# A batched matmul on one core: all loads first, all stores after, with every output kept on chip

## The chip, the cores and the metric

The kernel runs on one core of a Trainium2 chip. The metric is the device time of one execution in microseconds (us).

## The reference

```python
def setup_inputs():
    batch, m, k, n = 16, 512, 512, 512
    return {
        "a": np.random.randn(batch, k, m).astype(np.float32),
        "b": np.random.randn(batch, k, n).astype(np.float32),
    }

def reference(a, b):
    return np.matmul(a.transpose(0, 2, 1), b).astype(np.float32)
```

Per batch, 1 MiB of `a` and 1 MiB of `b` come in and 1 MiB goes out: 48 transfers of 1 MiB, 50.33 MB (33.55 in, 16.78 out).

## The kernel before

One queue (the sync engine, SP) issues every load and every store but one small first write. Loads run six batches ahead of stores (`LAG`). VectorE (DVE) casts each input to bfloat16, TensorE (PE) multiplies into the result memory PSUM, and ScalarE (ACT) evacuates that, which means that it copies the result into an output tile in the on-chip memory SBUF. HBM is the memory outside, where the inputs and the output are.

```python
    LAG = 6
    NL = 5            # float32 input slots
    NB = 2            # bfloat16 slots
    NO = LAG + 2      # output slots
    H = MO // 2
    ...
        def load(i):
            j = i % NL
            if i >= NL:
                nc.sync.wait_ge(s_acast, i - NL + 2)
            nc.sync.dma_start(a_ts[j][:], a_v[i]).then_inc(s_a[j], 16)
            nc.sync.dma_start(b_ts[j][:], b_v[i]).then_inc(s_b[j], 16)

        def store(i):
            if i == 0:
                nc.sync.wait_ge(s_w, 16)
            nc.sync.wait_ge(s_ev1, i + 1)
            nc.sync.dma_start(out_v[i], o_ts[i % NO][:]).then_inc(s_o[i % NO], 16)

        for i in range(LAG):
            load(i)
        for i in range(batch):
            if i + LAG < batch:
                load(i + LAG)
            store(i)
    ...   # DVE: cast a, cast b; PE: 16 matmuls a batch
        for i in range(batch):          # ACT
            if i >= NO:
                nc.scalar.wait_ge(s_o[i % NO], 16 * (i // NO))
            for h in range(H):
                nc.scalar.wait_ge(s_mm, H * i + h + 1)
                nc.scalar.copy(out=o_ts[i % NO][:, 2 * h:2 * h + 2, :],
                               in_=ps_ts[(i % NB) * H + h][:]
                ).then_inc(s_ev1 if h else s_ev0, 1)
```

So from the seventh batch of loads on the queue holds: load `a`, load `b`, store, load `a`, load `b`, store, and so on. The kernel in full:

## Time and profile before

| before | |
|---|---|
| time, median of the first 3 executions | 126.58 us (126.41 to 127.03) |
| span of the profiled execution | 124.4 us |
| bytes moved | 50.33 MB by the main queue |
| busy share of the span | PE 55%, DVE 32%, ACT 27%, DMA engines 97.1% |

These lines are from the page of the kernel before. The first is the busy time of PE, with its share of the span. The next three show the span in 40 slices: the granted PE clock in tenths, the busy share of the DMA engines in tenths, and what these moved. Then come the main DMA queue (packets, MB, share of 16 engines) and the three costliest kinds of work (busy us, mean ns of one, idle time before them and what ended it).

```profile
PE 68.8 (55%) x256; PEld 29.5 (24%) x256; DVE 39.3 (32%) x32; ACT 33.6 (27%) x33; POOL 0.4 (0%) x5
...
PEclk9999999999999996799855999586799859999655
DMA  3999999999999999999999999999999999999991
GB/s 47 424 429 424 424 424 421 424 421 424 424 414 424 432 421 432 419 424 419 429 408 427 432 419 429 427 427 424 421 432 427 421 419 421 421 421 427 437 419 42
...
q1 hardware_dynamic: 6912, 50.33, 97.1%
...
L100 PE MATMUL ps<-bbf,abf 128*128 128x512 bf16 x256 | 68.8, 430 | 42.1 <-PEq L97 42.1
L120 ACT COPY o<-ps 128x1024 f32<-128x1024 f32 x32 | 32.3, 1013 | 64.6 <-PE ps L100 64.6
...
L86 DVE CAST abf<-a 128x2048 bf16<-128x2048 f32 x16 | 19.6, 1227 | 48.6 <-DMA a<-in_a_dram 48.6
```

The DMA row is what to look at: 9 in every slice but the first and the last, at some 424 GB/s. The compute engines spend most of their time waiting, and the casts wait for DMA. This kernel is bound by its transfers. The Trainium skill, "HBM Reference", section "Specifications (TRN2)", gives about 358 GB/s as the per-core share and says that a core streaming alone reaches about 425; the 424 here agree with the latter.

The next lines are from the timeline of DVE: start, duration, engine, line, operation, and in brackets how long the engine was idle and what ended that. They are the `a` casts of batches 8 to 11, and those of batches 14 and 15.

```profile
50.76 1.23 DVE L86 CAST abf<-a 128x2048 bf16<-128x2048 f32 x1 [3.76 <-DMA a<-in_a_dram]
...
58.16 1.23 DVE L86 CAST abf<-a 128x2048 bf16<-128x2048 f32 x1 [3.76 <-DMA a<-in_a_dram]
...
66.03 1.23 DVE L86 CAST abf<-a 128x2048 bf16<-128x2048 f32 x1 [4.23 <-DMA a<-in_a_dram]
...
73.41 1.23 DVE L86 CAST abf<-a 128x2048 bf16<-128x2048 f32 x1 [3.74 <-DMA a<-in_a_dram]
...
95.60 1.23 DVE L86 CAST abf<-a 128x2048 bf16<-128x2048 f32 x1 [3.78 <-DMA a<-in_a_dram]
...
103.37 1.23 DVE L86 CAST abf<-a 128x2048 bf16<-128x2048 f32 x1 [4.13 <-DMA a<-in_a_dram]
```

The casts follow the transfers, so their starts are a clock for the stream. Most batches take 7.40 us (3.146 MB, 425 GB/s). Two take longer: 58.16 to 66.03 is 7.87 us, and 95.60 to 103.37 is 7.77 us. Together they are some 0.84 us over.

### The profile page before, as it was taken

The page shows a single profiled execution, that of the slowest core. Times are in us where ns is not written, and L with a number is a line of the kernel's source. Part 1 is how long each engine was busy: PE and PEld are TensorE (multiplying, and loading weights), DVE is VectorE, ACT ScalarE, POOL GpSimd, SP SyncE. Part 2 cuts the span into 40 slices and gives each one's busy share as a digit, 9 for nine tenths or more (in the row PEclk, how much of TensorE's full clock was granted, in tenths as well). Part 3 has the DMA queues.
Part 4 walks back from the last instruction along what each step waited for, and adds up shares of the span by engine and source line. Part 5 has one row for each costly group of instructions (what it writes and reads, how often), then busy time and mean ns, then how long its engine had stood idle before and what let it go on. Part 6 is the DMA issues. An engine that isn't in the chain of part 4 may idle for free. (4 is left out here: it accounts for less than half of the span.)

```text
span 124.4 us, 762 instructions
## 1 busy us (share of the span) xinstructions
PE 68.8 (55%) x256; PEld 29.5 (24%) x256; DVE 39.3 (32%) x32; ACT 33.6 (27%) x33; POOL 0.4 (0%) x5
## 2 busy tenths in 40 slices
PE   0007989595775907947099561957937095560000
PEld 0002344252342403323033220313323032220000
DVE  0055345534653061333403333061332503300000
ACT  0000564633524330425003360240325106060000
POOL 1000000000000000000000000000000000000000
PEclk9999999999999996799855999586799859999655
DMA  3999999999999999999999999999999999999991
GB/s 47 424 429 424 424 424 421 424 421 424 424 414 424 432 421 432 419 424 419 429 408 427 432 419 429 427 427 424 421 432 427 421 419 421 421 421 427 437 419 42
DMA packets 7056, 50.40 MB, mean 405 GB/s; under 512 B 784, under 2 KB 912, under 8 KB 912
## 3 DMA queue, kind: packets, MB, share of 16 engines
q1 hardware_dynamic: 6912, 50.33, 97.1%
q10 hardware_dynamic: 144, 0.07, 0.2%
HBM read 33.55 MB, written 16.84 MB: 405 GB/s over the span
## 5 line engine op out<-in xcount | busy, mean ns | idle before, releaser
L100 PE MATMUL ps<-bbf,abf 128*128 128x512 bf16 x256 | 68.8, 430 | 42.1 <-PEq L97 42.1
L120 ACT COPY o<-ps 128x1024 f32<-128x1024 f32 x32 | 32.3, 1013 | 64.6 <-PE ps L100 64.6
L100 PEld LDWEIGHTS ps<-bbf,abf 128*128 128x128 bf16 x256 | 29.5, 120 | 80.9 <-issue 63.3
L86 DVE CAST abf<-a 128x2048 bf16<-128x2048 f32 x16 | 19.6, 1227 | 48.6 <-DMA a<-in_a_dram 48.6
L88 DVE CAST bbf<-b 128x2048 bf16<-128x2048 f32 x16 | 19.6, 1227 | 19.1 <-DMA b<-in_b_dram 19.1
L120 ACT ACT_TABLE_LOAD x1 | 1.3, 1283 | 13.7 <-PE ps L100 13.7
L111 POOL MEMSET o<- 128x128 f32 x1 | 0.2, 204 | 0.5 <-SPq L57 0.5
L137 POOL MEMSET const-bfloat16-1.0<- 128x1 bf16 x1 | 0.1, 101 | 0.0
L137 POOL MEMSET const-uint8-127<- 128x1 uint8 x1 | 0.1, 101 | 0.0
L137 POOL MEMSET const-float32-0.0<- 128x1 f32 x1 | 0.1, 98 | 0.2 <-issue 0.2
L137 POOL MEMSET const-float32-1.0<- 128x1 f32 x1 | 0.1, 98 | 0.0
## 6 DMA issues: line engine op xcount, KB each, us to landing
a<-in_a_dram SPq DMA_DIRECT2D x16, 1024.0 KB, 22.2
b<-in_b_dram SPq DMA_DIRECT2D x16, 1024.0 KB, 24.3
out_dram<-o SPq DMA_DIRECT2D x16, 1024.0 KB, 26.1
out_dram<-o ACTq DMA_DIRECT2D x1, 64.0 KB, 5.0
```

The source lines that it names most:

```text
L86: nc.vector.tensor_copy(out=abf_ts[i % NB][:], in_=a_ts[i % NL][:]).then_inc(s_acast, 1)
L88: nc.vector.tensor_copy(out=bbf_ts[i % NB][:], in_=b_ts[i % NL][:]).then_inc(s_bcast, 1)
L100: mm = nc.tensor.matmul(ps_ts[u * H + mo // 2][:, mo % 2, :], a_m[:, ko, mo, :], bbf_ts[u][:, ko, :], start=(ko == 0), stop=(ko == KO - 1),)
L111: nc.gpsimd.memset(o_ts[0][:, 0, 0:P], 0.0).then_inc(s_z, 1)
L120: nc.scalar.copy(out=o_ts[i % NO][:, 2 * h:2 * h + 2, :], in_=ps_ts[(i % NB) * H + h][:]).then_inc(s_ev1 if h else s_ev0, 1)
L137: nc = _bacc.Bacc("TRN2", target_bir_lowering=False, num_devices=1)
```

## The change

The intent is to stop mixing loads and stores. All 16 outputs (16 tiles of 8 KB per partition) stay in SBUF, so stores can wait; to make room, the float32 input slots go from five to three. The queue issues all 32 loads and then all 16 stores. ACT never waits for an output slot. The diff, without its changes of blank lines:

```diff
-    LAG = 6
-    NL = 5
+    NL = 3
     NB = 2
-    NO = LAG + 2
     H = MO // 2
...
-    o_ts = [pool.tile([P, MO, N], f32, name=f"o{j}") for j in range(NO)]
+    o_ts = [pool.tile([P, MO, N], f32, name=f"o{j}") for j in range(batch)]
...
-    s_o = [tc.alloc_semaphore(f"s_o{j}") for j in range(NO)]
+    s_o = tc.alloc_semaphore("s_o")
...
-            nc.sync.dma_start(out_v[i], o_ts[i % NO][:]).then_inc(s_o[i % NO], 16)
+            nc.sync.dma_start(out_v[i], o_ts[i][:]).then_inc(s_o, 16)
 
-        for i in range(LAG):
+        for i in range(batch):
             load(i)
         for i in range(batch):
-            if i + LAG < batch:
-                load(i + LAG)
             store(i)
-        for j in range(NO):
-            nc.sync.wait_ge(s_o[j], 16 * len(range(j, batch, NO)))
+        nc.sync.wait_ge(s_o, 16 * batch)
...
         for i in range(batch):
-            if i >= NO:
-                nc.scalar.wait_ge(s_o[i % NO], 16 * (i // NO))
             for h in range(H):
                 nc.scalar.wait_ge(s_mm, H * i + h + 1)
                 nc.scalar.copy(
-                    out=o_ts[i % NO][:, 2 * h:2 * h + 2, :], in_=ps_ts[(i % NB) * H + h][:]
+                    out=o_ts[i][:, 2 * h:2 * h + 2, :], in_=ps_ts[(i % NB) * H + h][:]
                 ).then_inc(s_ev1 if h else s_ev0, 1)
```

## The prediction

> **What bounds the kernel now.** The DMA engines. In the page's slices the DMA row is at 9 from the second to the second-last slice, at 408 to 437 GB/s; queue q1 carries 50.33 MB in 97.1% of the 16 engines' span. 50.33 MB at 424 GB/s are 118.7 us of a 124.4 us span; the rest is latency at both ends. The Trainium skill, "DMA: Bandwidth & Descriptors", section "Bandwidth", gives 425 GB/s as measured for a large load; this trace agrees. No compute engine is near: PE 55%, DVE 32%, ACT 27%.
>
> **What the change does.** The same 48 transfers of 1 MB move. It removes the interleaving of loads and stores, the evacuation's wait for an output slot, and two of five input slots. A gain can only come from a better rate of unmixed transfers, as there are no gaps. The timeline already shows all three kinds of traffic:
> - loads alone (11 to 36 us): `a` casts start every 4.97 us, so 2.097 MB per batch come at 422 GB/s;
> - mixed (36 to 103 us): 7.40 us per batch of 3.146 MB, 425 GB/s, but two batches of 7.8 us;
> - stores alone (108 to 120 us): 427 to 434 GB/s, say 428.
>
> Afterwards: 33.55 MB at 422 are 79.5 us, 16.78 MB at 428 are 39.2 us, together 118.7 us, the time of now.
>
> **Do three slots hold the load stream?** Load i now waits for the `a` cast of batch i-2. In the present load-only stage that cast ends at 12.3 us for batch 1; what is then queued for three slots lands at 18.5 us, some 5 to 6 us later. First issue to landing was 5.1 us for 1 MB, of which 2.5 are transfer: 2.6 us of latency, so 3 us of margin. The casts need 2.45 us of each 4.97, PE 3.62 us (5.30 at half clock). The `a` cast at 30.98 us needs matmuls that ended at 28.6: 2.4 us of slack, still 0.7 if PE ran cold. PE's pauses in this stage are 1.35 us at clock 1.00; the cold batches come later, after pauses of 3.8 us. So PE should become steadier, which gains nothing.
>
> **Timeline expected.** The last load is issued at 72 to 73 us and lands near 83; a dozen outputs are ready by then, so stores follow at once. Compute ends near 90 us instead of 112. The tail is the same.
>
> **Predicted time: 126.5 us** (range 125.5 to 127.7); faster by over 2% 0.02, within 2% 0.95, slower by over 2% 0.03. On the critical path the change is worth about 0, perhaps 0.3 us either way.
>
> **What would show each step.** Right: DMA row at 9 throughout; about 422 GB/s to 83 us, about 428 afterwards; `a` casts 4.97 us apart to the last; PE clock near 1.0 until its last batch. Wrong: a slice under 9 between 10 and 80 us (three slots too few), casts over 5 us apart, a dip at the turn to stores, or stores under 420 GB/s over their whole 39 us.
>
> **What would make it wrong.** (1) Long store-only stretches slower than the 17 us seen now, through a backlog of writes. (2) The 16 engines drifting apart: with less in flight, a fast one could run dry while a load waits for the slowest. (3) A mixed stream that is really better: 425 against 422 suggests at most 0.4 us. (4) The two 7.8 us batches, 0.8 us together, belonging to the mixture: then after would be up to 0.8 us faster.

## The result, and the profile after

| | before | after |
|---|---|---|
| median of 6 executions | 126.62 us (126.41 to 127.03) | 125.84 us (125.61 to 126.07) |
| span of the profiled execution | 124.4 us | 123.6 us |
| last matmul ends | 110.9 us | 88.2 us |

The ratio of after to before is 0.9935, with a 95% interval of 0.9916 to 0.9954. A ratio is the mean time of one kernel's fast runs over that of the other's fast runs of the same rounds, so it is not quite the ratio of the medians quoted. The change is worth 0.6%: inside "within 2%", but clear of the noise, and 0.66 us better than the 126.5 us predicted.

The same lines of the page after:

```profile
PE 59.6 (48%) x256; PEld 28.0 (23%) x256; DVE 39.3 (32%) x32; ACT 33.6 (27%) x33; POOL 0.4 (0%) x5
...
PEclk9999999999999999999999999999985555555555
DMA  2999999999999999999999999999999999999993
GB/s 58 414 424 430 424 424 424 424 419 424 424 424 422 416 424 422 422 424 424 419 414 422 422 424 424 424 422 427 424 427 427 432 430 424 427 435 427 427 424 143
...
q1 hardware_dynamic: 6912, 50.33, 97.6%
...
L97 PE MATMUL ps<-bbf,abf 128*128 128x512 bf16 x256 | 59.6, 387 | 28.7 <-PEq L94 28.7
L115 ACT COPY o<-ps 128x1024 f32<-128x1024 f32 x32 | 32.3, 1013 | 42.0 <-PE ps L97 42.0
...
L83 DVE CAST abf<-a 128x2048 bf16<-128x2048 f32 x16 | 19.6, 1227 | 25.8 <-DMA a<-in_a_dram 25.8
```

The DMA row is again full. PE's matmuls now take 59.6 us in place of 68.8, because the granted clock stays high up to the end of compute, and the page gives nothing back for it: PE is not the bottleneck. The same `a` casts in the timeline after:

```profile
45.89 1.23 DVE L83 CAST abf<-a 128x2048 bf16<-128x2048 f32 x1 [1.32 <-DMA a<-in_a_dram]
...
50.87 1.23 DVE L83 CAST abf<-a 128x2048 bf16<-128x2048 f32 x1 [1.32 <-DMA a<-in_a_dram]
...
55.83 1.23 DVE L83 CAST abf<-a 128x2048 bf16<-128x2048 f32 x1 [1.32 <-DMA a<-in_a_dram]
...
60.81 1.23 DVE L83 CAST abf<-a 128x2048 bf16<-128x2048 f32 x1 [1.32 <-DMA a<-in_a_dram]
...
75.72 1.23 DVE L83 CAST abf<-a 128x2048 bf16<-128x2048 f32 x1 [1.32 <-DMA a<-in_a_dram]
...
80.69 1.23 DVE L83 CAST abf<-a 128x2048 bf16<-128x2048 f32 x1 [1.32 <-DMA a<-in_a_dram]
```

They are 4.96 to 4.98 us apart, with no long batch. So three slots hold the load stream, and the two long batches are gone. The waits of the DMA queue itself, after:

```profile
SPq L63 <- DVE abf L83: 57.9, 13, 8.0
SPq L63 <- DMA out_dram<-o: 25.0, 1, 25.0
SPq L70 <- ACT o L115: 2.2, 3, 1.4
```

The columns are the total, the number of times and the longest wait. The queue waits for a free slot 13 times (57.9 us in all) while transfers already issued keep the engines busy. The 25.0 us are the wait for the last store, after everything has been issued. The queue hardly waits for outputs (2.2 us against 29.6 before).

**Below the page: the 16 DMA engines one by one.** The trace holds 16 landings for every 1 MiB transfer, and 128 packets of 8 KB. It does not name the engine of a packet or a landing. I read the 16 landings as one per DMA engine, with 8 packets each: 8 packets of 0.309 us are 2.47 us, and the loads land 2.48 us apart. The following is worked out from these records, not an answer of the profile. "Typical" is the median of the 16 landings of the last store, "slowest" the last of them. "Slow packets" are those of 8 KB that took over 0.6 us, after the first 6 us.

```
                    last store lands, us           slow packets
kernel         typical  slowest  difference     number  longest us
before          121.89   122.91     1.02           7      0.94
after           122.02   122.24     0.22           0      0.33
```

Nearly every packet takes 0.309 to 0.321 us in both kernels. In before, seven packets of 6144 took 0.72 to 0.94 us: four at 64.6 us, one at 94.4 us and two at 101.7 us. What is lost once is not made up in this record. For loads, the gap between the slowest and the typical landing was 0.13 to 0.17 us from 38 us up to 63 us; the next load landed with 0.58 us, the loads up to 98 us kept 0.55 to 0.60, and the next one after the event at 101.7 us had 0.98 us. In after it stayed near 0.2 us. The typical engine of before was even 0.13 us earlier than that of after. So of the 0.82 us between the two spans, 0.67 us are the last landing: the gap of the slowest engine adds 0.80, and the lead of the typical one takes 0.13 back. The other 0.15 us lie after the last landing (1.50 us to the end of the span in before, 1.35 in after).

The questions left for the chip were: does this belong to the kernel or to one execution, and is it the mixture of loads and stores, or the fuller queue that five slots allow?

### The profile page after: what moved, and what is told of

The parts are those of the page before. It is cut to its first block, busy times and chain, and to the rows that moved or that the text cites. A ratio compares the mean times of both kernels' runs of the same rounds, so it can differ in the third digit from the quotient of the medians.

```text
span 123.6 us, 750 instructions
## 1 busy us (share of the span) xinstructions
PE 59.6 (48%) x256; PEld 28.0 (23%) x256; DVE 39.3 (32%) x32; ACT 33.6 (27%) x33; POOL 0.4 (0%) x5
## 3 DMA queue, kind: packets, MB, share of 16 engines
q1 hardware_dynamic: 6912, 50.33, 97.6%
## 5 line engine op out<-in xcount | busy, mean ns | idle before, releaser
L97 PE MATMUL ps<-bbf,abf 128*128 128x512 bf16 x256 | 59.6, 387 | 28.7 <-PEq L94 28.7
L97 PEld LDWEIGHTS ps<-bbf,abf 128*128 128x128 bf16 x256 | 28.0, 114 | 59.8 <-issue 37.6
L83 DVE CAST abf<-a 128x2048 bf16<-128x2048 f32 x16 | 19.6, 1227 | 25.8 <-DMA a<-in_a_dram 25.8
L85 DVE CAST bbf<-b 128x2048 bf16<-128x2048 f32 x16 | 19.6, 1227 | 19.3 <-DMA b<-in_b_dram 19.3
```

The lines of the kernel that those rows point to most:

```text
L83: nc.vector.tensor_copy(out=abf_ts[i % NB][:], in_=a_ts[i % NL][:]).then_inc(s_acast, 1)
L85: nc.vector.tensor_copy(out=bbf_ts[i % NB][:], in_=b_ts[i % NL][:]).then_inc(s_bcast, 1)
L97: mm = nc.tensor.matmul(ps_ts[u * H + mo // 2][:, mo % 2, :], a_m[:, ko, mo, :], bbf_ts[u][:, ko, :], start=(ko == 0), stop=(ko == KO - 1),)
```

## The experiments

**Theory 1:** loads and stores in one stream cause the slow packets. **Theory 2:** the full queue does (in before SP was held up to 5.94 us in a single issue of a `b` load, in after 0.87 in a load; but the stores of after fill the queue too, with 6.28 us in one issue at 78 us, and no packet is slow there). A third reading was chance: something outside the kernel in one execution.

All twelve runs are summed up here, with the same columns as above. The edits follow.

```
                    last store lands, us           slow packets       time, us
kernel         typical  slowest  difference     number  longest us   (executions)
before_again    121.84   123.19     1.34           7      0.83     126.7  (1)
mix16           121.89   122.87     0.98           6      0.93     126.34 (6)
mixrev          121.98   123.31     1.34          12      1.03     126.68 (1)
mixrev2         122.12   123.36     1.25          15      1.23     126.74 (1)
mixshift        121.77   123.14     1.37           6      0.86     126.51 (1)
mixshift2       121.80   123.40     1.59           8      1.19     126.76 (1)
fine            122.45   123.77     1.32          10      0.84     127.3  (6)
coarse5         121.97   122.26     0.29           0      0.45     125.91 (6)
after_again     122.02   122.48     0.45           0      0.33     125.79 (6)
sbstore         122.78   122.94     0.16           0      0.55     126.42 (1)
deep            130.80   130.95     0.15           0      0.35     134.38 (1)
tworings        130.37   130.45     0.09           1      0.61     133.91 (1)
```

### before_again: the kernel before, a second look

No edit.

> A second look at the kernel before, unchanged. In its first trace the median DMA engine finished the last store at 121.89 us and the slowest at 122.91 us (after: 122.02 and 122.24); the slowest fell back in two steps near 64.6 and 101.7 us, each time by some packets of 8 KB that took 0.72 to 0.94 us where all others take 0.31 to 0.32. If that belongs to the kernel (mixed loads and stores, or a full queue): again 2 to 4 such moments between 36 and 106 us, time 126.4 to 127.0. If it was a chance disturbance of that one execution: none, yet the time would then have to be near 125.9, which the six timed runs of before speak against.

Measured: 126.7 us, seven slow packets again, at 42.1, 94.2 to 94.4 and 101.5 us, and the slowest engine 1.34 us behind the typical one. So this belongs to the kernel: it came in both traces. The places are partly others than in the first trace: nothing over 0.6 us at 64.6 us, one at 42.1.

### mix16: the buffers of after, the order of before

```diff
+        LAG = 6
-        for i in range(batch):
+        for i in range(LAG):
             load(i)
         for i in range(batch):
+            if i + LAG < batch:
+                load(i + LAG)
             store(i)
```

> The changed kernel's buffers (16 outputs, three input slots), the order of before (six batches of loads, then one batch of loads and one store in turn). Theory 1, loads and stores in one stream cost the slow packets: as before, 126.6 us, 0.6 to 0.8 above the changed kernel, with packets of over 0.6 us in the mixed stage. Theory 2, a full queue (five slots, issue held up) costs them: as the changed kernel, 125.8 us, no packet over 0.6 us, since here a load is issued only when its slot is free and the queue never fills in the mixed stage.

Measured: 126.34 us (126.13 to 126.9); ratio to before 1.000, interval 0.997 to 1.003. Six slow packets. Three `a` casts in a row from its timeline show the long batch at 42 us:

```profile
36.05 1.23 DVE L86 CAST abf<-a 128x2048 bf16<-128x2048 f32 x1 [1.32 <-DMA a<-in_a_dram]
...
43.79 1.23 DVE L86 CAST abf<-a 128x2048 bf16<-128x2048 f32 x1 [4.11 <-DMA a<-in_a_dram]
...
51.20 1.23 DVE L86 CAST abf<-a 128x2048 bf16<-128x2048 f32 x1 [3.77 <-DMA a<-in_a_dram]
```

The first of these steps is 7.74 us, the second 7.41. The median is 0.2 us below that of before and 0.26 us below the 126.6 us of theory 1, but the ratio cannot be told from 1, and the trace looks like before. mix16 and after were not timed in the same rounds; their ratios to before, 0.997 to 1.003 and 0.9916 to 0.9954, do not overlap (that of after_again below, 0.9912 to 0.9977, touches the edge). With three slots and 16 outputs the gain is gone as soon as the order is the old one. So neither the slots nor the output tiles made it; the order did. Theory 2 said 125.8 and no slow packets; its issues here were held up 1.04 us at most in the mixed stage, and the slow packets came all the same.

### deep: a full queue without mixing

This gives a wrong result.

```diff
-    NL = 3
+    NL = 7
-    ... name=f"o{j}") for j in range(batch)]
+    ... name=f"o{j}") for j in range(8)]
-            nc.sync.wait_ge(s_ev1, i + 1)
-            nc.sync.dma_start(out_v[i], o_ts[i][:])...
+            nc.sync.wait_ge(s_ev1, batch)
+            nc.sync.dma_start(out_v[i], o_ts[i % 8][:])...
-                    out=o_ts[i][:, ...
+                    out=o_ts[i % 8][:, ...
```

> Wrong result on purpose: eight output tiles used twice, all stores held back until the last evacuation, so that seven input slots fit; all loads first. The queue is then full while loads run alone. Theory 2: packets over 0.6 us in the load stage, and the slowest DMA engine 0.4 us or more behind the median by its end. Theory 1: none, spread 0.3 us as in the changed kernel. In both the stores begin about 8 us late, so some 134 us in all.

Measured: 134.38 us. SP was held 2.1 to 6.3 us in most issues of the load stage, as these lines from its timeline show (start, duration):

```profile
37.83 0.43 SPq L63 DMA_DIRECT2D a<-in_a_dram  x1
38.30 6.32 SPq L64 DMA_DIRECT2D b<-in_b_dram  x1
44.66 2.14 SPq L63 DMA_DIRECT2D a<-in_a_dram  x1
46.84 2.13 SPq L64 DMA_DIRECT2D b<-in_b_dram  x1
```

Yet no load packet took over 0.33 us, and the gap between the slowest and the typical engine was 0.27 us at the end of the loads. A full queue alone made no slow packet here, and mix16 had slow packets without one. Theory 2 falls.

### fine: twice as many turns

The stores of mix16 are cut into halves of 64 partitions, one after each load.

```diff
+            for h in range(2):
+                if l < batch:                       # l = i + LAG
+                    (load_a if h == 0 else load_b)(l)
-                nc.sync.dma_start(out_v[i], o_ts[i][:]).then_inc(s_o, 16)
+                nc.sync.dma_start(
+                    out_v[i][64 * h:64 * h + 64], o_ts[i][64 * h:64 * h + 64]
+                ).then_inc(s_o, 16)
```

> As mix16, but each store is cut into two halves of 64 partitions and 512 KB, one after each 1 MB load: twice as many turns between loads and stores, the same bytes and the same 8 KB packets. Theory 1 with a price per turn: more slow packets than before has, 127.0 to 128 us. Theory 1 with a price per time spent mixed: as mix16, 126.6. Theory 2: 125.8.

Measured: 127.3 us, ratio to before 1.007 (1.004 to 1.010). The time is in the range of "a price per turn", but the trace says that this is not the reason. In the mixed stage, with twice the turns, no packet took over 0.41 us; all ten slow ones came after 107 us, where half stores ran with no loads, and the last half store landed 1.32 us after its typical engine. The slowest engine still fell back, by small steps, from 0.13 to 0.64 us behind the typical one by 107 us. This run is confounded: 64-partition transfers of 512 KB are themselves another thing. It shows that the price is not simply per turn, and that halving the stores doesn't pay. The typical engine is also 0.56 us later than in mix16, so not all of the loss is the slowest engine. Why half stores alone have slow packets is open.

### after_again: the changed kernel, a second look

No edit.

> The changed kernel, unchanged, beside the next three on one chip. Both theories: 125.6 to 126.1 us, 0.6 to 0.8 under before; no packet over 0.6 us after the first microseconds; the slowest DMA engine ends 0.2 us after the median one.

Measured: 125.79 us (125.66 to 125.85), ratio 0.9944 (0.9912 to 0.9977), no packet over 0.33 us. The gap at the end was 0.45 us rather than 0.2, a miss of the expectation. It was 0.18 us at the first load and 0.22 at the last, and grew to 0.43 over the first four stores. So the gap can grow without any slow packet, here after the turn from loads to stores; why is open. The scatter is a hint: six executions lie within 0.19 us, while the eleven of before on this chip go from 125.75 to 127.18. It is no proof, as the six of after in the first result span 0.46 us and the six of before 0.62.

### coarse5: one change from stores back to loads

```diff
+        LAG = 6
-        for i in range(batch):
+        for i in range(LAG):
             load(i)
-        for i in range(batch):
-            store(i)
+        for i in range(LAG, batch):
+            load(i)
+            if i in (10, 15):
+                for k in range(i - 10, i - 5):
+                    store(k)
+        for i in range(10, batch):
+            store(i)
```

> As mix16, but loads and stores alternate in blocks of five batches: one change from stores back to loads in place of nine. If the slow packets belong to loads that follow a store (theory 1): at most one place with slow packets, just after the first block of five stores, spread at the end under 0.7 us, time 125.7 to 126.2, near the changed kernel. If any order other than all loads first costs the whole 0.7 us: 126.4.

Measured: 125.91 us (125.63 to 126.76), ratio 0.997 (0.993 to 1.001); no slow packet, gap 0.29 us. The median and the trace lie near after_again (125.79 us), so anything but "all loads first" does not seem to cost the whole gain. But the interval also holds 1, and one execution of the six took 126.76 us, so the times do not settle it. As about a third of the turns in the mixed kernels show slow packets (below), a single turn without any proves little.

### sbstore: the same mixture without HBM writes

The kernel before with three input slots; a wrong result.

```diff
-    NL = 5
+    NL = 3
+    x_ts = [pool.tile([P, MO, N], f32, name=f"x{j}") for j in range(NO)]
-            nc.sync.dma_start(out_v[i], o_ts[i % NO][:]).then_inc(s_o[i % NO], 16)
+            nc.sync.dma_start(x_ts[i % NO][:], o_ts[i % NO][:]).then_inc(s_o[i % NO], 16)
```

> Wrong result on purpose: the order of before with three input slots, and each store goes to a tile in SBUF in place of HBM (only the first small write goes to out). Loads and stores share the DMA engines as in before, but there is no HBM write. If the slow packets need HBM writes beside HBM reads: none over 0.6 us, spread at the end 0.4 us. If they come from loads and stores sharing the DMA engines or the SBUF side: some, spread 0.9 us or more, as in before.

Measured: 126.42 us; no slow packet (longest 0.55 us), gap 0.16 us against 1.0 to 1.6 in the mixed kernels that write HBM. Its typical engine is 0.9 us later, since these copies come 2.48 us apart and stores to HBM 2.44; that is why the total is no test. In this one trace, two kinds of transfer that shared the DMA engines made no slow packet without HBM writes.

### mixrev and mixrev2: other addresses at the same places

mix16 from the last batch to the first; mixrev2 is unchanged from mixrev.

```diff
-            nc.sync.dma_start(a_ts[j][:], a_v[i])...
+            nc.sync.dma_start(a_ts[j][:], a_v[batch - 1 - i])...
             (b_v and out_v likewise)
```

> As mix16, but the batches are taken from the last to the first: the right result, the same order of loads and stores, other addresses at each place. In the three traces of mixed kernels slow packets came at 42.1 to 42.5, 64.6 to 64.8, 94.2 to 94.8 and 101.5 to 101.8 us, each time in a load of a that follows a store. If a pair of HBM addresses causes them, they move or vanish here; if the place in the stream or the time causes them, they come at the same times. Time in both cases 126.0 to 126.9.

> mixrev unchanged, a second look. In batch order the slow packets came in loads of a number 7, 10, 14 and 15 (three traces), in reverse order in the loads number 7, 9 and 13. If addresses decide: again near 42.3, 56.5 to 57.3 and 86.6 to 86.9 us, and not near 64.7, 94.4 or 101.6. If the places are drawn by chance each time: others than these.

Measured: 126.68 and 126.74 us. mixrev had slow packets at 42.3 to 42.5, 56.5 to 57.3 and 86.6 to 86.9 us. mixrev2 had them at 49.7 to 51.3, 57.2 to 57.3 and 72.5 to 72.6 us, and a single one at 7.6 us, where loads run alone. One place in three came again. Neither had any at 64.7, 94.4 or 101.6 us, where the three traces in batch order had most of theirs. This settles neither addresses nor chance. The chip is a rival that was not tested: before_again and mix16 ran on chip 0, mixrev on chip 3, mixrev2 and the next two runs on chip 5, and the record does not name the chip of the first trace of before.

### mixshift and mixshift2: only the written addresses moved

A wrong result.

```diff
-            nc.sync.dma_start(out_v[i], o_ts[i][:]).then_inc(s_o, 16)
+            nc.sync.dma_start(out_v[(i + 8) % batch], o_ts[i][:]).then_inc(s_o, 16)
```

> Wrong result on purpose: as mix16, but batch i is stored as batch i+8 (round the end). Loads read the same addresses at the same times as in mix16; only the written addresses differ. If the address that is read decides alone: slow packets near 42.3, 64.7, 94.5 and 101.6 us as in mix16. If the pair of read and written addresses decides: at other places. Time 125.9 to 127 either way.

> mixshift unchanged, a second look: the same places as in mixshift if addresses decide, others if chance does.

Measured: 126.51 and 126.76 us. mixshift: 49.9, 57.4 to 57.6, 72.2 and 89.0 us. mixshift2: 57.2 to 57.3 and 86.3 to 87.0 us. The loads read the same addresses at the same times as in mix16, whose slow packets came at 42.5, 64.7 and 94.5 to 94.8 us; none of the places agrees. If the chip does not matter, the address that is read does not decide alone. The two traces share one place of four and two, near 57.3 us, which mixrev and mixrev2 had as well, with loads from other addresses there. Whether addresses, the chip or only chance decide is left open.

**The seven mixed traces together** (before, before_again, mix16, mixrev, mixrev2, mixshift, mixshift2) have 61 slow packets. I put each to the load that was in flight by the landings: 55 of them fall in an `a` load that directly follows a store, 0.7 to 1.8 us after that store's typical landing. Five more fall in a `b` load after such a load, and one in the load-only start. Each trace has nine such turns from a store to a load; 20 of these 63 turns had at least one slow packet. What a slow packet waits for is not in the records.

### tworings: mixing packet by packet

All stores are issued by ACT, from a second queue, at once.

```diff
-        for i in range(batch):
-            store(i)
...
+            nc.scalar.wait_ge(s_ev1, i + 1)      # ACT, after the two copies of batch i
+            nc.scalar.dma_start(out_v[i], o_ts[i][:]).then_inc(s_o, 16)
```

> The changed kernel's buffers; all stores are issued by the scalar engine as soon as a batch is evacuated, so loads and stores stand in two queues and mix packet by packet from batch 0 on. If slow packets come with any mixture of HBM reads and writes (theory 1): over 0.6 us, more than the 4 to 12 of the mixed kernels so far. Time is no test here: the last batch's cast, matmuls, evacuation and store (1.2 + 3.6 or 5.3 + 1 + 2.5 + about 2 us) then lie behind the last load, and I estimate 130 to 134 us.

Measured: 133.91 us, and one slow packet (0.61 us) in place of more than 4 to 12: the expectation of theory 1 failed in this form. There are 28 packets over 0.45 us, though, against 11 in mix16 and none in after. All 28 are packets of loads (SP's queue) and lie between 19.6 and 21.7 us, after ACT has issued the first store at 17.4; later, with stores issued up to 126.6 us, the longest packet took 0.37 us. So the delays of this trace belong to one moment at the start of the mixture. (The gap of 0.09 us at the end says nothing, as the engines stood still before the last store.) Theory 1 in the words "any mixture of reads and writes gives slow packets" is too wide; whole 1 MiB stores followed by whole loads in one queue gave them in all seven mixed traces. The time was foreseen, and it is the second lesson of this kernel. These lines from its page show the end of the stream:

```profile
DMA  3999999999999999999999999999999999983033
GB/s 75 418 428 423 433 423 341 423 430 433 423 425 428 433 423 428 425 433 425 425 428 433 420 430 428 430 423 425 430 430 425 418 435 428 420 360 124 0 159 159
```

When stores are written as early as they can be, none are left to cover the last batch's cast, matmuls and evacuation: the DMA engines stand still near the end (a slice at 0). Both before and after avoid this, as each keeps at least seven stores for last.

## Why the prediction was right or wrong

- **What bounds the kernel now: the DMA engines.** Right. After, they are at 97.6%; PE got 9.2 us of busy time back and the total followed by 0.8 us, for another reason.
- **Do three slots hold the load stream?** Right that they do. The `a` casts are 4.96 to 5.05 us apart from the first to the last (the 5 us ones are among the first three); the last load was issued at 72.4 us (predicted 72 to 73) and landed at 83.1 (predicted near 83).
- **"PE should become steadier, which gains nothing."** Right. Every batch after the first took 3.62 us. The Trainium skill, "TensorE: Matmul & The Clock Gate", section "Part 1: The HAM clock gate", says that the clock halves after an idle window of about 3.4 us; this agrees in part: the four batches of before that followed pauses of 3.8 us took 4.9 to 6.6 us, and none did with the pauses of after, which are at most 1.37 us. But the batch of before at 84.7 us took 5.30 us after a pause of 2.08 us, so the prediction's "after pauses of 3.8 us" is not the whole of it, and in before_again one batch after a pause of 3.81 us took 3.62 us.
- **Compute ends near 90 us, and the tail is the same.** Right, nearly: 89.3 us with the last evacuation, and from the last landing to the end of the span 1.5 us before and 1.4 after.
- **The rates 422, 425 and 428 GB/s.** Right: load transfers land 2.48 us apart, stores 2.44, which is 1.0486 MB at 423 and 430 GB/s. The mixed stream was in fact a little better for a typical engine, by 0.13 us, inside the 0.4 us allowed in the list of doubts.
- **"together 118.7 us, the time of now", so 126.5 us.** The rates in the sum were right, and the total off by 0.66 us. The step that failed is "A gain can only come from a better rate of unmixed transfers, as there are no gaps", and with it "perhaps 0.3 us either way": the medians differ by 0.78 us, and no rate gave that. Mean rates give the time at which a typical engine is done. The kernel ends with its slowest, which lay 1.02 us behind in before (1.34 in the second trace) and 0.22 us in after (0.45). In all traces but one the span ended 1.35 to 1.50 us after the last landing (1.69 in fine). Doubt (4), "the two 7.8 us batches, 0.8 us together, belonging to the mixture", named the term and its size; it should have been in the main sum, as the one trace at hand already showed it twice. That the measured time still lies in the range of 125.5 to 127.7 us owes to the width of that range and not to the sum. mix16 showed that the term belongs to the order, deep that a full queue does not cause it.
- **Doubt (2), the engines drifting apart** was put to the wrong kernel: they drift in before, and hardly in after.
- **Doubt (1), long store stretches slowing down,** did not come: 2.43 to 2.47 us for each store over all 39 us.

Still open are why a load after a store sometimes has packets of two to four times the usual time, why only about a third of such turns are hit, why the gap grew without slow packets in after_again and fine, and why half-partition stores behave otherwise.

## What to carry to other kernels

In this kernel, bound by DMA with every slice full, rearranging transfers won back no more than the spread between the DMA engines: 0.6%, at the price of 16 output tiles in SBUF. To find such a loss, compare the last and the median of a transfer's 16 landings, or look for single batches that are longer than their neighbours in a steady stream; busy shares and GB/s didn't show it here. Keep enough stores for the end to cover the last batch's compute, whatever the order.

## What the Trainium skill lacked or had wrong

- "DMA: Bandwidth & Descriptors", section "Specifications", gives about 27 GiB/s per engine. Here an 8 KB packet took 0.309 us in the median, which is 8192 B / 0.309 us = 26.5 GB/s or 24.7 GiB/s; with 16 engines that makes the 424 GB/s measured. The figure of 425 GB/s in its section "Bandwidth" agrees.
- No page that I read says what loads and stores to HBM do to each other in one queue. Here 8 KB packets of a load after a 1 MiB store took up to 1.23 us in place of 0.31, in 20 of 63 such turns; without HBM writes the longest was 0.55 us.
- No page that I read gives a size for the spread of the 16 landings of one transfer. Here the last landing came 0.2 to 0.45 us after the median one in the unmixed kernel, and in the mixed ones 1.0 to 1.6 us after it, which is when the kernel ends.
- "DMA: Bandwidth & Descriptors", section "Rules for kernel authors", advises 128 partitions and at least 1 MiB per DMA. Nothing here speaks against it: with halves of 64 partitions the kernel took 127.3 us against 126.34 for whole stores (fine, mix16), though fine also has twice the turns, so the partitions alone are not shown to be the cause.
